# Column-tiled products, paired stores and earlier x in a batched matrix product on one core

## The chip, the cores and the metric

The kernel runs on one NeuronCore of a Trainium2 chip. The metric is device time in microseconds (us) of that core for one execution, as the median of several runs. Lower is better. Instruction times are given in nanoseconds (ns) where they are short.

## The reference

```python
batch, dim_i, dim_j, dim_k = 32, 256, 512, 384
out = np.einsum('bij,bjk->bik', x, y).astype(np.float32)   # x: 32x256x512, y: 32x512x384, float32
```

For each of 32 batches a 256x512 matrix is multiplied by a 512x384 matrix. x is 16.8 MB, y 25.2 MB and the output 12.6 MB, 54.5 MB in all.

## The kernel before, in words

**Operands.** TensorE contracts over the partitions, so j has to lie in the partitions for both operands. y comes that way from memory. x comes with i in the partitions and is transposed on TensorE, four batches at a time (a group, `Q = 4`), with an identity matrix, into PSUM (`t_ps`). Both operands are rounded to fp16 for the product. The j index is dealt out with a stride: partition q of y holds the four rows 4q to 4q+3 of a batch, so that each partition reads one contiguous run of 6 KB, and the transposes take the matching columns of x (`t::NJ`). For x, the 1024 rows of four batches are dealt out eight per partition, a run of 16 KB in each. For the output, partition m holds rows 2m and 2m+1 of one batch, a run of 3 KB.

**Functions.** `load(b)` (L59) issues the DMA of y for one batch (L69, 768 KB) and, for every fourth batch, first the DMA of x for that batch and the next three (L63, 2 MB). `transpose(q)` (L71) makes 32 transposes of 128x128 (L84) in eight sets of four. Each set fills one bank of `t_ps` and is copied to `xt_sb` as fp16, alternately by VectorE (L92) and by ScalarE (L94). `round_y(b)` (L97) copies y to fp16 in four pieces of 128x384, two on ScalarE (L102) and two on VectorE (L104). `multiply(b)` (L106) makes eight matmuls of 128x128 by 128x384 (L115), four for each of two output tiles `o_ps`. `collect(b)` (L124) copies the two tiles to `o_sb`, one on ScalarE (L128) and one on VectorE (L130). `store(b)` (L133) issues the DMA of one batch of output (L135, 384 KB).

**Order.** One Python loop writes the order of every engine's program by hand, one step for each batch (L141). A step s holds: the load of batch s+6, `collect(s-2)`, `multiply(s-1)`, the transposes of a group if s is a multiple of four, `round_y(s)`, and `store(s-2)`. Each engine runs its own part of this list strictly in that order. All DMAs are issued by SyncE (SP), so a load of a later step stands behind the store of the step before it. The framework gives the DMAs eight completion semaphores in rotation. A DMA is issued only when the DMA eight places before it has landed.

**Buffers.** There are 3 buffers for x, 10 for y, 4 for rounded y, 2 for transposed x, 10 for outputs, and in PSUM 4 banks for transposes and 4 for products.

Of the kernel before, what the change touches and what calls it, by code (L numbers as in the profile page):

```python
# [1 line left out]

# [5 lines left out]


MM_DT = mybir.dt.float16  # L10
F32 = mybir.dt.float32
P = 128


Q = 4

LAG = 8

ON_ACT = ()


@with_exitstack
def kernel(
    ctx: ExitStack,
    tc: tile.TileContext,
    x: bass.AP,
    y: bass.AP,
    out: bass.AP,
):
    nc = tc.nc  # L30

    B, I, J = x.shape
    _, _, K = y.shape

    NI = I // P
    NJ = J // P


    R = Q * NI
    PQ = P // Q  # L40

    const_pool = ctx.enter_context(tc.tile_pool(name="const", bufs=1))
    x_pool = ctx.enter_context(tc.tile_pool(name="x_pool", bufs=3))
    y_pool = ctx.enter_context(tc.tile_pool(name="y_pool", bufs=10))
    yr_pool = ctx.enter_context(tc.tile_pool(name="yr_pool", bufs=4))
    xt_pool = ctx.enter_context(tc.tile_pool(name="xt_pool", bufs=2))
    o_pool = ctx.enter_context(tc.tile_pool(name="o_pool", bufs=10))
    tpsum_pool = ctx.enter_context(tc.tile_pool(name="tpsum", bufs=4, space=bass.MemoryType.PSUM))
    opsum_pool = ctx.enter_context(tc.tile_pool(name="opsum", bufs=4, space=bass.MemoryType.PSUM))


    keep = tc.keep_in_program_order

    identity = const_pool.tile([P, P], F32)
    make_identity(nc, identity)

    x_of, y_of, yr_of, xt_of, ps_of, o_of = {}, {}, {}, {}, {}, {}

    def load(b):  # L59
        if b % Q == 0:  # L60
            x_of[b // Q] = x_pool.tile([P, R, J], F32, name="x_sb")
            keep(
                nc.sync.dma_start(  # L63
                    out=x_of[b // Q],
                    in_=x[b : b + Q].rearrange("g (p r) j -> (g p) r j", r=R),
                )
            )
        y_of[b] = y_pool.tile([P, NJ, K], F32, name="y_sb")
        keep(nc.sync.dma_start(out=y_of[b], in_=y[b].rearrange("(q t) k -> q t k", q=P)))  # L69

    def transpose(q):  # L71

        x_sb = x_of.pop(q)
        xt_of[q] = xt_pool.tile([P, Q, NJ, NI, PQ, Q], MM_DT, name="xt_sb")
        n = 0
        for t in range(NJ):
            for e in range(NI):  # L80
                t_ps = tpsum_pool.tile([P, Q, Q, PQ], F32, name="t_ps")
                for h in range(Q):
                    keep(
                        nc.tensor.transpose(  # L84
                            t_ps[:, h].rearrange("c g p -> c (g p)"),
                            x_sb[:, h * NI + e, t::NJ],
                            identity,
                        )
                    )
                dst = xt_of[q][:, :, t, e].rearrange("c g p h -> c h g p")  # L90
                if n % 2 == 0:
                    keep(nc.vector.tensor_copy(dst, t_ps))  # L92
                else:
                    keep(nc.scalar.copy(dst, t_ps))  # L94
                n += 1

    def round_y(b):  # L97
        y_sb = y_of.pop(b)
        yr_of[b] = yr_pool.tile([P, NJ, K], MM_DT, name="y_r")
        for t in range(NJ):  # L100
            if t % 2 == 0:
                keep(nc.scalar.copy(yr_of[b][:, t], y_sb[:, t]))  # L102
            else:
                keep(nc.vector.tensor_copy(yr_of[b][:, t], y_sb[:, t]))  # L104

    def multiply(b):  # L106
        xt_sb, y_r = xt_of[b // Q][:, b % Q], yr_of.pop(b)
        ps_of[b] = [
            opsum_pool.tile([P, K], F32, name=f"o_ps_{e}", tag="o_ps")
            for e in range(NI)  # L110
        ]
        for t in range(NJ):
            for e in range(NI):
                keep(
                    nc.tensor.matmul(  # L115
                        ps_of[b][e],
                        xt_sb[:, t, e].rearrange("c p h -> c (p h)"),
                        y_r[:, t],
                        start=(t == 0),
                        stop=(t == NJ - 1),  # L120
                    )
                )

    def collect(b):  # L124
        o_of[b] = o_pool.tile([P, NI, K], F32, name="o_sb")
        for e in range(NI):
            if e % 2 == 0:
                keep(nc.scalar.copy(o_of[b][:, e], ps_of[b][e]))  # L128
            else:
                keep(nc.vector.tensor_copy(o_of[b][:, e], ps_of[b][e]))  # L130
        del ps_of[b]

    def store(b):  # L133
        eng = nc.scalar if b in ON_ACT else nc.sync
        keep(eng.dma_start(out=out[b].rearrange("(m e) k -> m e k", m=P), in_=o_of.pop(b)))  # L135


    ahead = LAG - 2
    for b in range(ahead):
        load(b)  # L140
    for s in range(B + 2):  # L141
        if s + ahead < B:
            load(s + ahead)
        if s >= 2:
            collect(s - 2)
        if 1 <= s <= B:
            multiply(s - 1)
        if s < B and s % Q == 0:
            transpose(s // Q)
        if s < B:  # L150
            round_y(s)
        if s >= 2:
            store(s - 2)


# [1 line left out]
_INS = ['x', 'y']  # L157
_OUTS = [((32, 256, 384), 'float32')]


# [23 lines left out]
```

## Time and profile before

| what | value |
|---|---|
| median of 8 runs | 136.34 us (136.09 to 136.47) |
| the profiled execution: its own time | 136.15 us |
| the profiled execution: span from first to last instruction | 134.4 us |
| data moved | 54.53 MB in 72 DMAs, 406 GB/s over the span |
| packets of the data queue | 10368, their time is 98.1% of 16 DMA engines' span |
| busy: TensorE matmul, ScalarE, VectorE | 64%, 59%, 54% |

The span is 1.75 us shorter than the profiled execution's own time, which also holds what lies before the first and after the last recorded instruction. A busy share is an average over the whole span. The line of DMA digits gives the share of the 16 DMA engines that was at work in each fortieth of the span. In the list of queues, a packet is one contiguous run moved by one of the 16 DMA engines; runs of 4 bytes are the engines' completion marks, 16 for each DMA.

### The profile page before, as it was taken

How to read it: one execution, taken by the hardware profiler on the slowest of the kernel's cores; microseconds unless marked ns; L12 is line 12 of the kernel's file. 1: busy time of each engine (PE TensorE's matmuls, PEld its weight loads, DVE VectorE, ACT ScalarE, POOL GpSimd, SP SyncE). 2: the span in 40 equal slices, each digit the busy share in tenths (PEclk: the TensorE clock that was granted, in tenths of full speed). 3: DMA queues.
4: the chain of work that ended last, by engine and by line, in shares of the span. 5: the costliest groups of instructions: out<-in, count | busy, mean ns of one | idle time of the engine just before them, and what ended most of it. 6: DMA issues, size and time to landing. Idle time of an engine off the chain costs nothing.

```text
span 134.4 us, 1539 instructions
## 1 busy us (share of the span) xinstructions
PE 86.5 (64%) x512; PEld 64.3 (48%) x512; DVE 73.2 (54%) x128; ACT 79.6 (59%) x129; POOL 0.7 (1%) x6
## 2 busy tenths in 40 slices
PE   0049499869667809769195895949259492785900
PEld 0049358635654409644195454825159250883500
DVE  0007955976497404966078371977028870497610
ACT  3006994996399503996059770998009990289710
POOL 2000000000000000000000000000000000000000
PEclk9999999999999995999959599999968999689997
DMA  4999999999999999999999999999999999999993
GB/s 107 424 402 419 448 411 419 423 440 407 412 417 449 432 396 419 423 437 422 408 422 428 448 424 406 420 416 448 416 409 419 423 462 399 415 424 412 414 414 125
DMA packets 10375, 54.62 MB, mean 406 GB/s; under 512 B 1152, under 2 KB 1152, under 8 KB 9344
## 3 DMA queue, kind: packets, MB, share of 16 engines
q1 hardware_dynamic: 10368, 54.53, 98.1%
q8 instruction: 4, 0.07, 0.2%
q14 instruction: 3, 0.02, 0.0%
HBM read 41.94 MB, written 12.58 MB: 406 GB/s over the span
## 4 chain that ended last, share of the span: by engine, by line
DMA 86%; PE 5%; issue 1%; SPq 1%; DVE 1%; ACT 0%; DVEq 0%
DMA y_sb<-in_y_dram 47%; DMA x_sb<-in_x_dram 21%; DMA out_dram<-o_sb 19%; PE o_ps L115 4%; PE t_ps L84 1%; SPq L69 1%; ACT y_r L102 0%; DVE o_sb L130 0%; SPq L63 0%; DVE y_r L104 0%; SPq L135 0%; DVEq L130 0%
## 5 line engine op out<-in xcount | busy, mean ns | idle before, releaser
L94 ACT CAST xt_sb<-t_ps 128x512 f16<-128x512 f32 x32 | 39.4, 1370 | 44.1 <-PE t_ps L84 43.9
L92 DVE CAST xt_sb<-t_ps 128x512 f16<-128x512 f32 x32 | 39.6, 1331 | 41.0 <-PE t_ps L84 41.0
L84 PE MATMUL t_ps<-identity,x_sb 128*128 128x128 f32 x256 | 41.8, 330 | 25.7 <-DMA x_sb<-in_x_dram 25.7
L115 PE MATMUL o_ps<-y_r,xt_sb 128*128 128x384 f16 x256 | 44.9, 334 | 15.5 <-ACT y_r L102 15.5
L84 PEld LDWEIGHTS t_ps<-identity,x_sb 128*128 128x128 f32 x256 | 39.3, 215 | 29.2 <-issue 27.9
L115 PEld LDWEIGHTS <-xt_sb 128*128 128x128 f16 x256 | 25.7, 100 | 33.8 <-issue 19.0
L102 ACT CAST y_r<-y_sb 128x384 f16<-128x384 f32 x64 | 30.2, 528 | 1.3 <-DMA y_sb<-in_y_dram 1.3
L130 DVE COPY o_sb<-o_ps 128x384 f32<-128x384 f32 x32 | 17.8, 556 | 13.2 <-PE o_ps L115 13.2
L104 DVE CAST y_r<-y_sb 128x384 f16<-128x384 f32 x64 | 19.9, 354 | 0.9 <-DMA y_sb<-in_y_dram 0.9
L128 ACT COPY o_sb<-o_ps 128x384 f32<-128x384 f32 x32 | 15.5, 484 | 2.4 <-PE o_ps L115 2.4
L94 ACT ACT_TABLE_LOAD x1 | 1.3, 1283 | 0.7 <-PEq L168 0.7
masks.py:199 POOL TENSOR_SCALAR_AFFINE_SELECT identity<-identity 128x128 f32<-128x128 f32 x1 | 0.3, 294 | 0.1
masks.py:197 POOL MEMSET identity<- 128x128 f32 x1 | 0.2, 205 | 0.3 <-POOLq L168 0.3
L168 POOL MEMSET const-bfloat16-1.0<- 128x1 bf16 x1 | 0.1, 102 | 0.0
L168 POOL MEMSET const-uint8-127<- 128x1 uint8 x1 | 0.1, 102 | 0.0
L168 POOL MEMSET const-float32-0.0<- 128x1 f32 x1 | 0.1, 99 | 0.2 <-issue 0.2
L168 POOL MEMSET const-float32-1.0<- 128x1 f32 x1 | 0.1, 99 | 0.0
## 6 DMA issues: line engine op xcount, KB each, us to landing
y_sb<-in_y_dram SPq DMA_DIRECT2D x32, 768.0 KB, 15.0
x_sb<-in_x_dram SPq DMA_DIRECT2D x8, 2048.0 KB, 14.2
out_dram<-o_sb SPq DMA_DIRECT2D x32, 384.0 KB, 14.1
```

The costliest lines, as they stand in the source:

```text
L69: keep(nc.sync.dma_start(out=y_of[b], in_=y[b].rearrange("(q t) k -> q t k", q=P)))
L84: nc.tensor.transpose(t_ps[:, h].rearrange("c g p -> c (g p)"), x_sb[:, h * NI + e, t::NJ], identity,)
L92: keep(nc.vector.tensor_copy(dst, t_ps))
L94: keep(nc.scalar.copy(dst, t_ps))
L102: keep(nc.scalar.copy(yr_of[b][:, t], y_sb[:, t]))
L104: keep(nc.vector.tensor_copy(yr_of[b][:, t], y_sb[:, t]))
L115: nc.tensor.matmul(ps_of[b][e], xt_sb[:, t, e].rearrange("c p h -> c (p h)"), y_r[:, t], start=(t == 0), stop=(t == NJ - 1),)
L128: keep(nc.scalar.copy(o_of[b][:, e], ps_of[b][e]))
L130: keep(nc.vector.tensor_copy(o_of[b][:, e], ps_of[b][e]))
L168: nc = _bacc.Bacc("TRN2", target_bir_lowering=False, num_devices=1)
```

## The change

The kernel now works in units of two batches (`G = 2`), so that the loop has 16 steps instead of 32, with `LAG = 4` units.

- **Products** are made for two batches side by side. An output tile of 128 partitions holds 64 partitions of one batch above 64 of the other. Each matmul has 64 columns of weights and writes 64 partitions; two matmuls in a row go to the two halves of the same PSUM bank. There are 512 matmuls of 64 columns instead of 256 of 128, and four tiles for each unit.
- **Stores** take two batches in one DMA of 768 KB, with a run of 6 KB in each partition instead of two stores with runs of 3 KB.
- **Loads** of y take two batches in one DMA of 1.5 MB, except in the first and the last unit, which keep two single loads. x of a group is loaded with the last unit of the group before, ahead of its y, which is two batches sooner in the queue than before. x of the first group is loaded after the y of batch 0.
- **Transposes** of a group are made at the end of the step before the group's first unit, after that step's `round_y`. Those of the first group are made in step 0. Their layout differs: a set holds two output tiles with two row sets each, and the copy to `xt_sb` writes with a step of 2 elements over 128 positions instead of a step of 4 over runs of 32.
- **Buffers** hold two batches each, and their number is halved: 5 for y, 2 for rounded y, 5 for outputs.

```diff
-LAG = 8
+G = 2
+LAG = 4
...
+    def load(u):
+        if (u + 1) * G % Q == 0 and u + 1 < U:
+            load_x((u + 1) * G // Q)
+        y_of[u] = y_pool.tile([P, G, NJ, K], F32, name="y_sb")
+        n = 1 if u in (0, U - 1) else G
+        for g in range(0, G, n):
+            b = u * G + g
...
+                    out=y_of[u][:, g : g + n],
+                    in_=y[b : b + n].rearrange("g (q t) k -> q g t k", q=P),
...
+            if b == 0:
+                load_x(0)
...
-        xt_of[q] = xt_pool.tile([P, Q, NJ, NI, PQ, Q], MM_DT, name="xt_sb")
+        xt_of[q] = xt_pool.tile([P, NJ, NE, Q * PQ, H], MM_DT, name="xt_sb")
...
-                dst = xt_of[q][:, :, t, e].rearrange("c g p h -> c h g p")
+                dst = xt_of[q][:, t, e : e + 2].rearrange("c f p h -> c f h p")
...
+        for e in range(NE):
+            o_ps = opsum_pool.tile([P, K], F32, name="o_ps")
+            ps_of[u].append(o_ps)
+            for t in range(NJ):
+                for g in range(G):
+                    a = (u * G + g) % Q
...
+                            o_ps[g * M : (g + 1) * M],
+                            xt_sb[:, t, e, a * PQ : (a + 1) * PQ].rearrange("c p h -> c (p h)"),
+                            y_r[:, g, t],
...
+                out=out[u * G : (u + 1) * G].rearrange("g (m e) k -> (g m) e k", e=NE),
...
+    for s in range(U + 2):
+        if s + ahead < U:
+            load(s + ahead)
+        if s == 0:
+            transpose(0)
         if s >= 2:
             collect(s - 2)
-        if 1 <= s <= B:
+        if 1 <= s <= U:
             multiply(s - 1)
-        if s < B and s % Q == 0:
-            transpose(s // Q)
-        if s < B:
+        if s < U:
             round_y(s)
+        if (s + 1) * G % Q == 0 and s + 1 < U:
+            transpose((s + 1) * G // Q)
         if s >= 2:
             store(s - 2)
```

## The prediction

> **What bounds the kernel now.** I read the slices of the page first, then its queues and its chain.
>
> ```profile
> DMA  4999999999999999999999999999999999999993
> GB/s 107 424 402 419 448 411 419 423 440 407 412 417 449 432 396 419 423 437 422 408 422 428 448 424 406 420 416 448 416 409 419 423 462 399 415 424 412 414 414 125
> DMA packets 10375, 54.62 MB, mean 406 GB/s; under 512 B 1152, under 2 KB 1152, under 8 KB 9344
> q1 hardware_dynamic: 10368, 54.53, 98.1%
> q8 instruction: 4, 0.07, 0.2%
> DMA 86%; PE 5%; issue 1%; SPq 1%; DVE 1%; ACT 0%; DVEq 0%
> ```
>
> The DMA engines are full in all but the first and last slice. The chain is 86% DMA. So the waits of TensorE for x, 25.7 us in the list of waits, cost nothing: what they delay isn't what the queue lacks. The end is a sum of packet times, plus a head before the queue runs and a tail after it empties. The windows view (columns: stretch, length, busy time and count of PE, PEld, DVE, ACT, POOL, then clock, DMA share, GB/s) gives the rate by kind of traffic.
>
> ```profile
> 4.00:19.00 15.00, 8.38 (x48) 7.15 (x49) 7.02 (x11) 7.75 (x11) 0.00 (x0) 1.00 1.01 427
> 69.00:85.00 16.00, 12.58 (x69) 8.86 (x67) 9.36 (x17) 10.35 (x17) 0.00 (x0) 0.83 1.02 424
> 129.00:130.00 1.00, 0.00 (x0) 0.00 (x0) 0.00 (x0) 0.00 (x0) 0.00 (x0) 1.00 1.03 415
> 131.00:132.00 1.00, 0.00 (x0) 0.00 (x0) 0.00 (x0) 0.00 (x0) 0.00 (x0) 1.00 0.70 283
> ```
>
> Almost only loads: 427. Loads and stores in turn: 424. Stores alone, with their 3 KB runs: 415. Nothing here runs far from the rest. SP's timeline shows the period of a group of four batches by its x issues.
>
> ```profile
> 36.45 0.33 SPq L63 DMA_DIRECT2D x_sb<-in_x_dram  x1
> ...
> 52.47 0.33 SPq L63 DMA_DIRECT2D x_sb<-in_x_dram  x1
> ...
> 84.64 0.33 SPq L63 DMA_DIRECT2D x_sb<-in_x_dram  x1
> ...
> 100.66 0.33 SPq L63 DMA_DIRECT2D x_sb<-in_x_dram  x1
> ```
>
> That is 16.05 us a group (64.21 over four), for 6.82 MB, hence 425 GB/s. By the end of the chain, the products of the last four batches run in one piece and the last copy ends at 128.3, while the queue is full to 131:
>
> ```profile
> 122.36 5.37 PE o_ps L115 x32
> 127.73 0.02 issue
> 127.76 0.56 DVE o_sb L130
> ```
>
> [...] the packet records have medians of 611, 234, 121 and 9 ns for 16 KB, 6 KB, 3 KB and a completion mark. From 3 KB to 6 KB it is 113 ns, so 8 ns of each data packet are fixed. [...] The trace of before has no tiled product. [...] The copies of L92 and L94 write 2 bytes in steps of 8[...] and still take 1331 and 1370 ns against 556 and 484 ns for 384 elements of L130 and L128; the trace shows the step to be dear. [...] four fetches of 16 KB on q8 for 1024 TensorE instructions.
>
> **The change part by part.**
>
> *Stores in runs of 6 KB, fewer DMAs.* 4096 packets of 3 KB become 2048 of 6 KB: 4096 x 121 - 2048 x 234 = 16.4 us of engine time, over 16 engines 1.02 us. DMAs go from 72 to 42, which takes away 480 marks of 9 ns, 0.27 us. The face value is -1.3 us. But packets overlap: stores alone fill 103%. By the landings in the trace a 3 KB store takes 0.945 us, two of them 1.89, and a y load with 6 KB runs 1.885. If a 6 KB store costs what a y load costs, the gain is 16 x 0.005 = 0.1 us. If it keeps the overlap of about 4 ns a packet, it is 8 x 230 + 9 = 1.85 us, and the gain 0.6 us. Against this: x 4.90 us, four y of 1.885 and four stores of 0.945 make 16.22, and the group takes 16.05. The turns from store to load win 0.17 us, four in a group, and the change leaves two: up to 8 x 0.085 = 0.7 us given back. Merged y loads save 14 of the marks, 0.13 us, already in the 0.27. Together -1.3 to +0.6; I take -0.25 us, since 0.6 + 0.27 - 0.7 is about -0.2 and the face value pulls down.
>
> *Products.* A full product is issued every 167 ns in a run (5.37 us for 32). A unit of two batches needs 16 now, 2.7 us, and 32 narrow ones later. If two run at once, 2.7 us again; if not, 5.4 us. Weight loads, 100 ns for 128 columns, become two narrower ones per pair, between 2 x 50 and 2 x 100 ns. I take 170 ns a pair, bounds 167 and 334. In mid-run a unit has 8.0 us of DMA time and TensorE also has 2.7 us of transposes for it (half of 5.4), so even 5.4 fits, barely; the queue covers it. At the end it does not (below).
>
> *Copies out of PSUM.* Counts of y copies and output copies are the same. The transposed copies write in steps of 4 bytes: between the 1331 ns of now and 741 ns (556 x 512/384). I take 1331; nothing depends on it in mid-run, as ScalarE's 5.8 us per unit lie under 8.0 us of DMA.
>
> *x two batches sooner, transposes a step sooner.* Per group one x DMA moves past two y in SP's queue; bytes and number stay. What stood behind x waits 4.9 us longer, and that is y that ScalarE and VectorE round in the step before the transposes. The TensorE waits for x go; next late is the same full queue, so this is worth 0. At the start y of batch 0 comes ahead of x and the first transposes shift from 8.7 to about 10.5 us; the first stores have ten batches of load ahead of them in the queue, over 30 us, so it costs 0 (bounds -0.3 and +0.3, for the order of the first packets).
>
> *Added waits.* Four output banks hold one unit only, so a product waits for the copy of the unit before, and behind it stand TensorE's next transposes. SP's loads still stand behind stores. At such a point three later loads are queued, over 5 us of work after the longest series of copies, and eight larger DMAs may be outstanding: 0.
>
> *Instructions.* TensorE goes from 1024 to 1536 instructions, hence about six fetches instead of four. Each took about 1.0 us on one DMA engine and made that engine about 1.1 us later than the rest in the landings. So far each hit another engine; then two more cost 0. If two meet on one engine: +1.1.
>
> *The end.* Call T the landing of the last y. Behind it are five stores of 1.89 us: the queue ends at T+9.4. On the other side: y of the last unit is rounded by T+1.35 (four casts of about 0.5 on ScalarE, two of them earlier), the copy that frees its first bank ends at T+1.85, products 2.7, last copy 0.6: the store is issued at T+5.2. An issue takes 1.0 us to its first packet (0.74 to 1.73 at the start), 1.9 to move and 0.3 to land: T+8.4. That hides by 1.0 us. A second chain: copies of the last transposes end at about T-4.5, and from T-4 three units of products follow: T-4 + 3m + 0.7 + 3.2. It reaches T+9.4 when a unit takes m = 3.2 us, 198 ns a pair.
>
> Sum: 136.15 - 0.25 = 135.9 for the profiled execution; its median stands 0.19 higher: 136.1 us.
>
> **The rivals.**
>
> *Narrow products don't overlap fully* (slower). Price: from 198 ns a pair on, three times the excess. At 250 ns m = 4.0 and the end comes 2.4 us later, 138.5; at 334 ns m = 5.4 and 6.6 us later, 142.7. [...] Against: full products hide loads of 100 ns now, and quicker copies would start the chain 2 us sooner.
>
> *Two instruction fetches on one DMA engine*: 136.1 + 1.1 = 137.2. For it: six fetches instead of four. Against: the four were spread.
>
> *Face value*: all of the packets' fixed time is won, 136.34 - 1.3 = 135.0. Against: 6 KB loads are no faster than 3 KB stores.
>
> *The stores aren't longer*: if a packet were cut at 3 KB, only marks would go, less the lost turns, 136.6. Against: y has 6 KB packets.
>
> **How the numbers follow.** Forecast 0.59 (own range 135.3 to 136.7), narrow products 0.20, fetches 0.10, face value 0.06, uncut gain absent 0.05. A measurement of this kernel can tell about 0.2%, 0.27 us, from no change. The forecast's gain of 0.25 lies at that bound: of its 0.59, faster 0.28, same 0.24, slower 0.07. With the rivals: faster 0.34, same 0.24, slower 0.42. The range 135.2 to 138.6 leaves out some 0.06 below and 0.1 above.
>
> **What would show it.** Right: data packets of 6 KB at about 230 ns, a group period of 15.9 to 16.1 us, DMA digits still 9 to the last two slices, no wait for x on TensorE, a unit's products within 3.2 us. Wrong: DMA digits that fall before the last store, a unit's products of 4 us or more, one DMA engine landing over 2 us after the others, or a period clearly off 16 us.

## The result, and the profile after

| | before | after |
|---|---|---|
| median | 136.28 us (31 runs beside these) | 137.27 us (136.78 to 137.59, 11 runs) |
| ratio to before, 95% interval | | 1.0070 (1.0059 to 1.0081) |
| the profiled execution: its own time, span, difference | 136.15, 134.4, 1.75 us | 136.97, 134.9, 2.07 us |

The changed kernel is about 1.0 us slower where 0.25 us faster was forecast. Part of that, 0.3 us, lies outside the span.

From the page of the changed kernel, the lines that answer to those of before:

```profile
DMA  4999999999999999999999999999999999999992
GB/s 153 450 393 462 395 421 434 456 380 415 284 459 405 414 426 425 446 408 414 425 429 463 394 417 426 451 415 405 423 425 443 428 403 425 423 428 417 420 397 109
DMA packets 7848, 54.64 MB, mean 405 GB/s; under 512 B 672, under 2 KB 672, under 8 KB 6816
q1 hardware_dynamic: 7840, 54.53, 97.6%
q8 instruction: 6, 0.10, 0.3%
q14 instruction: 2, 0.02, 0.0%
```

The queue is still full throughout, and the packets are as many as reckoned: 6144 of 6 KB, 1024 of 16 KB, 672 marks. But look at the eleventh value of the second line: 284 GB/s in a slice whose DMA digit is 9. There the engines were at work and moved two thirds of the usual bytes; the 6 KB packets that start between 35.0 and 35.5 us took 541 ns on average, against 234. The windows view shows that place in both kernels, first before, then after (the last two columns are DMA share and GB/s).

```profile
33.00:37.00 4.00, 2.79 (x20) 2.26 (x19) 1.59 (x2) 1.11 (x2) 0.00 (x0) 1.00 1.01 415
```

```profile
33.00:37.00 4.00, 1.18 (x9) 1.11 (x9) 2.76 (x7) 3.00 (x6) 0.00 (x0) 1.00 1.01 303
...
53.00:69.00 16.00, 10.94 (x99) 9.61 (x99) 7.25 (x17) 7.58 (x16) 0.00 (x0) 0.93 1.01 424
69.00:85.00 16.00, 11.13 (x100) 9.46 (x99) 7.11 (x17) 7.61 (x17) 0.00 (x0) 0.92 1.01 426
...
129.00:130.00 1.00, 0.00 (x0) 0.00 (x0) 0.28 (x1) 0.00 (x0) 0.00 (x0) 1.00 0.83 344
130.00:131.00 1.00, 0.00 (x0) 0.00 (x0) 0.00 (x0) 0.00 (x0) 0.00 (x0) 1.00 1.00 418
```

In mid-run the rate is that of before: 424 and 426. The trace also records when each of the 16 DMA engines finished its share of a DMA, without naming the engine; these records are called the landings below, and "first" and "last engine" are the first and the last of the 16. By the first engine, the x loads of the fourth and the eighth group land 64.14 us apart (43.47 and 107.61). Before it is the same 64.14 us (48.68 and 112.82), so 16.03 us a group in both. At 129 us the share dips to 0.83: DMA engines that run ahead have nothing left until the last store arrives (it is issued at 129.34, and the first engine lands the store before it at 129.79). The engine that lands last isn't among them: it lands the last two stores at 132.04 and 133.86, 1.82 us apart, no more than the stores before them.

The parts that the forecast had sized on the compute side, first the groups of before, then those of the changed kernel:

```profile
L115 PE MATMUL o_ps<-y_r,xt_sb 128*128 128x384 f16 x256 | 44.9, 334 | 15.5 <-ACT y_r L102 15.5
L94 ACT CAST xt_sb<-t_ps 128x512 f16<-128x512 f32 x32 | 39.4, 1370 | 44.1 <-PE t_ps L84 43.9
L92 DVE CAST xt_sb<-t_ps 128x512 f16<-128x512 f32 x32 | 39.6, 1331 | 41.0 <-PE t_ps L84 41.0
```

```profile
L132 PE MATMUL o_ps<-y_r,xt_sb 128*64 128x384 f16 x512 | 46.5, 339 | 6.0 <-DVE o_sb L147 4.3
L132 PEld LDWEIGHTS <-xt_sb 128*64 128x64 f16 x512 | 36.3, 114 | 15.8 <-issue 7.1
L109 ACT CAST xt_sb<-t_ps 128x512 f16<-128x512 f32 x32 | 22.6, 737 | 20.6 <-PE t_ps L101 20.6
L107 DVE CAST xt_sb<-t_ps 128x512 f16<-128x512 f32 x32 | 22.7, 733 | 20.7 <-PE t_ps L101 20.7
```

and from its chain, the last unit:

```profile
124.74 0.04 DVE y_r L120
...
125.89 2.81 PE o_ps L132 x32
128.69 0.02 issue
128.72 0.56 DVE o_sb L147
```

512 products of 64 columns are busy for 46.5 us where 256 of 128 columns took 44.9, and a unit's 32 run in 2.81 us, 176 ns a pair, against 167 ns for one full product before. So two of them do run at once: in the trace of the last unit the two of a pair start 3 to 4 ns apart, and the pairs, after the first, 162 to 163 ns apart, as single full products did before (median 162 ns). The copies to `xt_sb` fell from 1331 and 1370 to 733 and 737 ns.

### The profile page after: what moved, and what is told of

It reads as the page before. It is cut to its first block, busy times and chain, and to the rows that moved or that the text cites. A ratio compares the mean times of both kernels' runs of the same rounds, so it can differ in the third digit from the quotient of the medians.

```text
span 134.9 us, 1958 instructions
## 1 busy us (share of the span) xinstructions
PE 88.9 (66%) x768; PEld 75.1 (56%) x768; DVE 56.2 (42%) x128; ACT 62.5 (46%) x129; POOL 0.7 (1%) x6
## 4 chain that ended last, share of the span: by engine, by line
DMA 72%; PE 10%; DVE 6%; SPq 4%; ACT 2%; issue 2%; DVEq 0%; ACTq 0%
DMA y_sb<-in_y_dram 72%; PE t_ps L101 7%; PE o_ps L132 3%; DVE y_r L120 3%; DVE xt_sb L107 2%; SPq L66 2%; SPq L82 2%; ACT o_sb L145 1%; DVE o_sb L147 1%; SPq L152 1%; ACT xt_sb L109 0%; DVEq L120 0%; ACTq L145 0%
## 5 line engine op out<-in xcount | busy, mean ns | idle before, releaser
L101 PE MATMUL t_ps<-identity,x_sb 128*128 128x128 f32 x256 | 42.6, 333 | 33.7 <-DVE xt_sb L107 20.0
L101 PEld LDWEIGHTS t_ps<-identity,x_sb 128*128 128x128 f32 x256 | 38.8, 214 | 37.4 <-DVE xt_sb L107 21.1
L132 PE MATMUL o_ps<-y_r,xt_sb 128*64 128x384 f16 x512 | 46.5, 339 | 6.0 <-DVE o_sb L147 4.3
L118 ACT CAST y_r<-y_sb 128x384 f16<-128x384 f32 x64 | 28.3, 520 | 43.5 <-DMA y_sb<-in_y_dram 43.5
L132 PEld LDWEIGHTS <-xt_sb 128*64 128x64 f16 x512 | 36.3, 114 | 15.8 <-issue 7.1
L120 DVE CAST y_r<-y_sb 128x384 f16<-128x384 f32 x64 | 18.6, 353 | 42.4 <-DMA y_sb<-in_y_dram 42.2
L109 ACT CAST xt_sb<-t_ps 128x512 f16<-128x512 f32 x32 | 22.6, 737 | 20.6 <-PE t_ps L101 20.6
L107 DVE CAST xt_sb<-t_ps 128x512 f16<-128x512 f32 x32 | 22.7, 733 | 20.7 <-PE t_ps L101 20.7
L147 DVE COPY o_sb<-o_ps 128x384 f32<-128x384 f32 x32 | 16.9, 550 | 10.0 <-PE o_ps L132 9.9
L145 ACT COPY o_sb<-o_ps 128x384 f32<-128x384 f32 x32 | 14.1, 493 | 1.2 <-PE o_ps L132 1.2
```

Of the source, the lines that this page charges most:

```text
L101: nc.tensor.transpose(t_ps[:, f, h], x_sb[:, h * NE + e + f, t::NJ], identity)
L118: keep(nc.scalar.copy(yr_of[u][:, g, t], y_sb[:, g, t]))
L120: keep(nc.vector.tensor_copy(yr_of[u][:, g, t], y_sb[:, g, t]))
L132: nc.tensor.matmul(o_ps[g * M : (g + 1) * M], xt_sb[:, t, e, a * PQ : (a + 1) * PQ].rearrange("c p h -> c (p h)"), y_r[:, g, t], start=(t ...
L145: keep(nc.scalar.copy(o_of[u][:, e], ps_of[u][e]))
L147: keep(nc.vector.tensor_copy(o_of[u][:, e], ps_of[u][e]))
```

## The experiments

Three theories were set against each other. The **fetch theory**: two more TensorE instruction fetches make one DMA engine late. The **stall theory**: the slow packets at 33 to 37 us are the loss. The **end theory**: the last store comes too late. Each kernel was compared with the kernel before on the same chip; medians of that were 136.28 to 136.30.

**again.** The changed kernel, unchanged.

> The changed kernel unchanged, to see which parts of its profile repeat. Stall theory: the slow packets at 33 to 37 us (about 1.1 us of extra packet time on every DMA engine) belong to the kernel and are there again, at the same place. Chance: they are gone, and the time then falls to 136.3 or less. Fetch theory: six instruction fetches again, and the slowest DMA engine lands over 2 us after the fastest, with or without the slow packets. Time 137.0 to 137.5.

Measured: 137.23 (ratio 1.0079, 1.0060 to 1.0099). Slow packets at the same place, six fetches, the last landing 2.4 us after the first for the second last store. The slow packets belong to the kernel.

**b_yfirst.** The kernel before with y of batch 0 ahead of x.

```diff
     def load(b):
+        if b == 0:
+            y_of[b] = y_pool.tile([P, NJ, K], F32, name="y_sb")
+            keep(nc.sync.dma_start(out=y_of[b], in_=y[b].rearrange("(q t) k -> q t k", q=P)))
         if b % Q == 0:
...
-        y_of[b] = y_pool.tile([P, NJ, K], F32, name="y_sb")
-        keep(nc.sync.dma_start(out=y_of[b], in_=y[b].rearrange("(q t) k -> q t k", q=P)))
+        if b > 0:
+            y_of[b] = y_pool.tile([P, NJ, K], F32, name="y_sb")
+            keep(nc.sync.dma_start(out=y_of[b], in_=y[b].rearrange("(q t) k -> q t k", q=P)))
```

> The kernel before with one thing changed: y of batch 0 is loaded ahead of the first x. In the landings the fastest DMA engine of the changed kernel had lost 2.4 us to the head instead of 2.9. If the order of the first two loads does that, this kernel is 0.4 to 0.6 us faster than before; if it is chance or due to something else, no difference.

Measured: 136.56 (1.0016, 1.0003 to 1.0029), with a wide spread, from 135.84 to 137.07. The expectation failed, and showed why: the tenth DMA lands 0.52 us sooner on the first engine (27.29 against 27.81), and by the nineteenth that is gone (43.76 against 43.81). Between them, y packets between 32 and 36 us average 271 ns against 237 in the kernel before. So the order of two DMAs brings slow packets into a kernel that had none. The windows view of this kernel, where the kernel before has 415 GB/s:

```profile
33.00:37.00 4.00, 4.00 (x29) 3.19 (x28) 2.58 (x5) 2.06 (x5) 0.00 (x0) 1.00 0.99 376
```

**b_extra_pe.** The kernel before with 512 more TensorE instructions: 256 small products, each with its weight load.

```diff
+        for t in range(NJ):
+            for e in range(NI):
+                keep(
+                    nc.tensor.matmul(
+                        ps_of[b][e][:, :32],
+                        xt_sb[:, t, e].rearrange("c p h -> c (p h)"),
+                        y_r[:, t, :32],
+                        start=True,
+                        stop=True,
+                    )
+                )
```

> The kernel before with 256 extra small products (32 columns) into banks that the real products then overwrite: 1536 TensorE instructions and so six instruction fetches instead of four, as in the changed kernel, with loads, stores and order untouched. TensorE has over a third of its time free. Fetch theory: 0.5 to 1.2 us slower than before, and the slowest DMA engine lands more than 2 us after the fastest. Stall theory and end theory: no difference.

Measured: 136.52 (1.0015, 1.0007 to 1.0024), six fetches, no slow packets. Slower by 0.24 us, below the expected band. The two more fetches (or the other effects of those products, which this run doesn't separate) cost this much here, a quarter of what the changed kernel lost.

**a_fullwidth.** The changed kernel with full-width products; the transposed layout and the products of before, the rest as changed.

```diff
+        for g in range(G):
+            a = (u * G + g) % Q
+            for e in range(2):
+                o_ps = opsum_pool.tile([P, K], F32, name="o_ps")
+                ps_of[u].append(o_ps)
+                for t in range(NJ):
+                    keep(
+                        nc.tensor.matmul(
+                            o_ps,
+                            xt_sb[:, a, t, e].rearrange("c p h -> c (p h)"),
+                            y_r[:, g, t],
...
-                out=out[u * G : (u + 1) * G].rearrange("g (m e) k -> (g m) e k", e=NE),
-                in_=o_of.pop(u),
+                out=out[u * G : (u + 1) * G].rearrange("g (m e) k -> m g e k", e=2),
+                in_=o_of.pop(u).rearrange("m (g e) k -> m g e k", e=2),
```

> The changed kernel with the products made at full width again (256 of 128 columns, the transposed layout of before), units of two batches, loads, order and buffers as changed. A store is still one DMA of two batches, with two runs of 3 KB in each partition. 1024 TensorE instructions, four fetches. Fetch theory: 0.5 to 1 us faster than the changed kernel, near 136.3. Stall theory (the start with 12 MB of loads before any store): stays near 137.2, with slow packets at 33 to 37 us. End theory (last store issued late): stays near 137.2, with the DMA digits falling before the last store.

Measured: 137.53 (1.0085, 1.0067 to 1.0103), four fetches, slow packets as before. So neither two more fetches nor narrow products are the main loss: without both the kernel is no faster. The run doesn't price them by themselves, since its stores are back at runs of 3 KB.

**a_xfirst.** The changed kernel with x ahead of y of batch 0.

```diff
+        if u == 0:
+            load_x(0)
         y_of[u] = y_pool.tile([P, G, NJ, K], F32, name="y_sb")
...
-            if b == 0:
-                load_x(0)
```

> The changed kernel with x of the first group loaded ahead of y of batch 0 again, and nothing else. Order theory (y first is what makes the DMA engines meet slow packets when y of batches 8 and 9 is loaded): no slow packets at 33 to 37 us, the head 0.5 us later, and 0.2 to 0.5 us faster than the changed kernel, 136.7 to 137.0. Unit theory (they come from the 12 MB of loads in a row): slow packets stay and the time rises to 137.5 or more.

Measured: 136.40 (1.0007, 0.9996 to 1.0017), 0.85 us faster than the changed kernel, more than expected. No slow packets at 33 to 37 us, by the windows view of this kernel:

```profile
33.00:37.00 4.00, 1.22 (x8) 1.02 (x7) 2.43 (x6) 2.84 (x6) 0.00 (x0) 0.80 1.01 416
```

By this one edit, the order of the first two loads is most of the loss.

**a_y1.** The changed kernel (y first) with y loads of one batch.

```diff
-        n = 1 if u in (0, U - 1) else G
+        n = 1
```

> The changed kernel with every y load for one batch again: 56 DMAs, seven for each semaphore, instead of 42. Epilogue theory: the 56th DMA is on the last semaphore, so SP's final waits end with the last landing (0.05 us from landing to the end waits instead of 0.25), and SP's longer program meets its instruction fetch during the run and not after the end (time outside the span 1.75 instead of 2.05): about 0.5 us faster, 136.7 to 136.8. If the time outside the span has nothing to do with SP's program: it stays at 2.05, and the gain is 0.2 at most. Slow packets stay.

Measured: 136.99 (1.0055, 1.0039 to 1.0070). The time outside the span went from 2.07 to 1.76 us in the median of the runs, as the epilogue theory had it, and from the last landing to the end of the span from 1.00 to 0.83 us. The gain in the median is 0.26 us, half of what was expected: in this profile the last engine is 3.0 us behind the first from 36 us on, against 2.3 to 2.5 in the changed kernel, which may have taken the rest back.

**a_y1_xfirst.** Both of the above.

> Both of the above: x first, and y loads for one batch. If the two theories hold and add up, 136.2 to 136.6, within 0.3 us of the kernel before; what is left is the two more TensorE instruction fetches (0.24 us in the run with extra products). If it stays above 136.9, another cause is missing.

Measured: **136.03** (0.9986, 0.9975 to 0.9997), below the expected band and faster than the kernel before. It is the fastest of all kernels tried.

**b_74.** The kernel before with two y loads cut in two.

```diff
+        src = y[b].rearrange("(q t) k -> q t k", q=P)
+        if b in (20, 21):
+            keep(nc.sync.dma_start(out=y_of[b][:, : NJ // 2], in_=src[:, : NJ // 2]))
+            keep(nc.sync.dma_start(out=y_of[b][:, NJ // 2 :], in_=src[:, NJ // 2 :]))
+        else:
+            keep(nc.sync.dma_start(out=y_of[b], in_=src))
```

> The kernel before with the y loads of batches 20 and 21 cut in two DMAs each: 74 DMAs instead of 72, the same bytes, so that the last DMA falls on the second of the eight completion semaphores. Epilogue theory: SP waits for it first and then goes through the others, 0.2 us slower (136.45 to 136.5), with more waits between the last landing and the end of the span (1.04 us instead of 0.83). Otherwise: no difference.

Measured: 136.55 (1.0018, 1.0004 to 1.0031), 0.25 us slower. From the last landing to the end of the span it is 1.00 us (134.03 to 135.03) against 0.83. The sign is as expected; 0.17 us of it is in the final waits, and the rest could be the two more DMAs with shorter runs. SP's list of waits shows the two endings, first of the kernel before, then of b_74:

```profile
SPq L179 <- DMA out_dram<-o_sb: 4.7, 5, 1.1
```

```profile
SPq L184 <- DMA out_dram<-o_sb: 4.6, 1, 4.6
```

Before, SP waits five times for one store after the other, and the last landing ends it. In b_74 one wait of 4.6 us holds the last landing, and SP goes through three more semaphores after it, about 0.06 us each. The changed kernel does the same, and has the same 1.00 us. (The expectations gave 1.04 us for it, from a rounded span.)

**a_rev.** The changed kernel (y first), groups taken from memory in reverse order; shown for y, x and the output go the same way.

```diff
             b = u * G + g
+            c = (B // Q - 1 - b // Q) * Q + b % Q
...
-                    in_=y[b : b + n].rearrange("g (q t) k -> q g t k", q=P),
+                    in_=y[c : c + n].rearrange("g (q t) k -> q g t k", q=P),
```

> The changed kernel, y first, with the groups of four batches taken in reverse order from memory: the fifth y load then reads batches 20 and 21, not 8 and 9, and all else is as it was. Address theory (those rows of y are slow to read in that state): the slow packets of 33 to 37 us go or move. Place theory (it is this point of the stream, whatever is read): y packets still take about 290 to 310 ns on average between 32 and 36 us, against 234 later. Time about 137.2 in the second case, 136.4 to 136.7 in the first.

Measured: 136.95 (1.0057, 1.0037 to 1.0077). Slow packets at 34 to 36 us, up to 561 ns on average in half a microsecond. Which rows are read is not the cause.

**a_pad.** The changed kernel with one useless load of 768 KB near the start.

```diff
+            if b == 1:
+                pad = pad_pool.tile([P, NJ, K], F32, name="pad")
+                keep(nc.sync.dma_start(out=pad, in_=y[0].rearrange("(q t) k -> q t k", q=P)))
```

> The changed kernel, y first, with one more load of 768 KB that nothing uses, after y of batch 1: everything behind it comes 1.9 us later in the stream. Stream theory: the slow packets come with the load of batches 8 and 9, now at 35.5 to 39 us. Clock theory (something at a fixed time after the start): they stay at 33 to 37 us, on other loads. Time about 139.1 in both.

Measured: 139.21 (1.0213, 1.0197 to 1.0229). The slow packets came at 35.5 to 37.5 us, 1.9 us later, again in the load of batches 8 and 9. The clock theory falls.

**a_late_store.** The changed kernel with the first store behind one more unit of loads.

```diff
-        if s >= 2:
+        if s == 3:
+            store(0)
+        if s >= 3:
             store(s - 2)
```

> The changed kernel, y first, with the first store issued one unit later, behind the loads of x of the fourth group and of y of batches 10 and 11. First-store theory (the slow packets hit the load that stands right before the first store): y of batches 8 and 9 is read at 234 to 240 ns a packet, and the slow packets come some 8.7 us later, with batches 10 and 11, at 42 to 46 us. Place theory (it is the end of the first run of loads, whatever follows): they stay at 33 to 37 us. Time 137.0 to 137.5 in both.

Measured: 136.93 (1.0061, 1.0039 to 1.0083). The slow packets moved with the store, by the windows view of this kernel:

```profile
33.00:37.00 4.00, 3.47 (x28) 3.11 (x25) 2.75 (x7) 3.00 (x6) 0.00 (x0) 1.00 1.07 445
...
42.00:45.00 3.00, 3.00 (x36) 2.44 (x31) 0.31 (x1) 0.04 (x1) 0.00 (x0) 1.00 1.02 347
```

445 GB/s where the changed kernel had 303, and 347 at 42 to 45 us, where batches 10 and 11 are loaded. So the slow packets are again in the load right before the first store. The store itself was issued only 2.3 us later than in the changed kernel (28.59 against 26.30 us); what moved by one unit is its place in the queue, and the slow packets went with the place.

**a_full_y1_x.** The kernel a_y1_xfirst with the full-width products and 3 KB runs of a_fullwidth (the same edits, not repeated).

> The kernel with x first and single y loads, but with full-width products and runs of 3 KB in the stores: 1024 TensorE instructions and four fetches. It holds against that one what the column tiling is worth by itself. If 6 KB runs are worth their face value, it is 1.0 us slower, 137.0. If they are worth about 0.3 us and the two more fetches cost 0.25, no difference: 135.9 to 136.2.

Measured: 136.43 (1.0016, 1.0007 to 1.0025), 0.40 us slower than a_y1_xfirst, between the two expectations. So narrow products with 6 KB runs gain 0.40 us net, together with their two more fetches.

**a_x2.** a_y1_xfirst with the first x in two DMAs of 8 KB runs.

```diff
-        keep(
-            nc.sync.dma_start(
-                out=x_of[q],
-                in_=x[q * Q : (q + 1) * Q].rearrange("g (p r) j -> (g p) r j", r=R),
-            )
-        )
+        src = x[q * Q : (q + 1) * Q].rearrange("g (p r) j -> (g p) r j", r=R)
+        n = R // 2 if q == 0 else R
+        for r in range(0, R, n):
+            keep(nc.sync.dma_start(out=x_of[q][:, r : r + n], in_=src[:, r : r + n]))
```

> The kernel with x first and single y loads, with x of the first group loaded by two DMAs of 8 KB runs (and y of batches 14 and 15 by one, to keep 56 DMAs). If the 0.5 us that y first saved at the head come from shorter first packets, about half of it is won without the slow packets: 135.7 to 135.9. If shorter first packets are themselves what brings the slow packets, 136.3 to 137.

Measured: 136.36 (1.0006, 0.9993 to 1.0020), 0.33 us slower than a_y1_xfirst, with slow packets at 34 to 36 us of about half the size. So y as such isn't needed: a first DMA of x with shorter runs brings slow packets too, fewer of them. (Two y loads of batches 14 and 15 are merged in this run, to keep 56 DMAs.)

## Why the prediction was wrong

**The step that failed** is the one on the start: "the first stores have ten batches of load ahead of them in the queue, over 30 us, so it costs 0 (bounds -0.3 and +0.3, for the order of the first packets)". The reasoning looked at who waits, and nobody does. The runs showed 0.85 us: 137.25 with y first (between 137.27 and 137.23, the two medians of the changed kernel), 136.40 with x first. Among the kernels with single y loads the same order costs 0.96 us (136.99 and 136.03), and in the kernel before only 0.28 (b_yfirst), so its price depends on the kernel.

The order saves less than it loses. In the landings of the changed kernel the first engine is 0.56 us ahead after the head (32.17 for the eighth DMA, 32.73 in a_xfirst), the last engine only 0.16 us. The next DMA, the load of two batches ahead of the first store, takes 4.51 us on the first engine and 5.30 us on the last, against 3.76 and 3.72 in a_xfirst. So the first engine loses 0.75 us and the last 1.58 us, and the last engine ends the program. Counted above 234 ns each, the 6 KB packets that start between 20 and 50 us cost every engine 1.29 us on average in the changed kernel, 1.00 in its second run and 0.28 in a_xfirst, a difference of the size of the loss. That the slow packets go with the load before the first store, and not with time or the rows, is shown by a_pad, a_rev and a_late_store.

That they account for all of the 0.85 us isn't shown: it is a difference of medians, and the last landings of the two profiled executions are only 0.13 us apart. The profiled execution of a_xfirst took 136.85 us, 0.45 above its median, and in it the last engine loses another 0.5 us near the end, on one store (2.31 us where the others take 1.82 to 1.88), with an instruction fetch at 126.4 us just before.

**What stays open** is why a first DMA with shorter runs does this. In the y-first profiles the last two engines land the first DMA 0.83 to 1.2 us after the first engine, in a_x2 0.87 and 1.11, in the other x-first ones 0.5 to 0.8. So the slow packets go with engines that fall apart at the start; whether the one causes the other is not shown. One could guess that engines which already store disturb those that still load. The record speaks against it. Where stores have packets of 3 KB, they can be told from loads: in a_fullwidth 35 of the 36 packets over 350 ns between 28 and 38 us start before the first store packet (36.18 us), in b_yfirst 18 of 25 (33.91 us).

**A second term was missing**: what the number of DMAs does to the end of the program. With y loads of one batch, a_xfirst became a_y1_xfirst and won 0.37 us, where the forecast had 0.13 us in favour of merging. With y first it was 0.26. Two causes can be seen. The 72 DMAs of before, and 56, end on the last of eight semaphores and 42 don't, so SP goes through other waits after the last landing: from landing to the end of the span 1.00 us against 0.83. And the time outside the span is 1.92 to 2.12 us in the seven profiles whose page shows two fetches on q14, and 1.77 to 1.86 us in the eight that show three or four; the medians are about 2.0 and 1.8. The page of a_y1_xfirst:

```profile
q8 instruction: 6, 0.10, 0.3%
q14 instruction: 3, 0.02, 0.0%
```

With 42 DMAs SP has 75 recorded instructions, with 56 it has 89, with 72 it has 121. In the trace the third fetch comes at 97.8 us before, at 132.3 us in a_y1_xfirst, and at 136.7 us, behind the end of the span, in the changed kernel. That this fetch is SP's, and that it makes the 0.2 to 0.3 us, fits all fifteen profiles, but was not tried by itself.

**The steps that held.** *The packets*: -0.25 us was forecast for the body of the change. With the two losses undone, a_y1_xfirst stands at -0.27 us by the medians (ratio 0.9986, so -0.19 us); narrow products with longer runs gain 0.40 us net, with the fetches and the quicker transposed copies in it. The face value of 1.3 us was rightly cut down. In mid-run the landings show none of the gain (64.14 us for four groups in both kernels); that the lost turns took it back there, as the forecast had it, fits this but was not tried by itself. At the end, where only stores are left, a 6 KB store takes the last engine 1.83 us (1.85 was reckoned with the overlap kept) and two 3 KB stores took 1.89; over five stores that is 0.3 us. *Products*: 170 ns a pair forecast, 176 measured; the rival of products that don't overlap is out. That two would run at once was the author's estimate: the trace of before, without a tiled product, shows neither this nor the contrary. *The last unit*: from T, 124.71, the last store was forecast at T+5.2 and issued at T+4.6. It hides on the engine that ends, but not on the first ones, which stood still; the forecast had taken the engines as one. *Transposed copies*: 733 ns, just under the lower bound of 741, worth nothing as said. *Waits for x* went but for a rest: five waits of 13.8 us are left in all, 10.2 of them before the first transpose. *Group period*: 16.03 us, within the 15.9 to 16.1 named.

Of the signs of being wrong that were named, one came: the last engine lands 2.3 to 2.5 us after the first, where 2 us was the limit; the kernel before was already at 2.0. It had been meant for two fetches on one engine. In the changed kernel the lag grows from 0.85 to 1.7 us at the first fetch, as it did before (0.7 to 1.8), and to 2.5 us in the load with the slow packets.

**The rival of the fetches** forecast 137.2, the time that was measured, but for the wrong reason: the two more fetches are worth 0.24 us in b_extra_pe, and with four fetches a_fullwidth is no faster. That its figure was hit is luck.

**The sum**, in medians: +0.85 for the order of the first loads, +0.37 for merged loads with what they do to the end, -0.27 for all else, in all +0.95, against 0.95 to 0.99 measured. This is a way of dividing the difference and no independent proof: the last term is what was left over, and undone in the other order the first two are 0.26 for merging and 0.96 for the order.

## What to carry to other kernels

In this kernel, whose DMA queue is always full, the last of the DMA engines set the end (its last landing is at 133.86 us of a span of 134.9). In one like it, look at slow stretches in the rate where the DMA digits are still 9, and not only at waits. The order of the first two loads was worth 0.3 to 1 us here though nothing waits for them: try it alone before it is mixed with other changes. And when the number of DMAs changes, look at the end: which wait of SP holds the last landing, and whether an instruction fetch has moved behind the span.

## What was not expected of the hardware

- Packets of 6 KB took up to 580 ns on average over half a microsecond (a_pad), against 234, in the load ahead of the first store, if the program's first DMA had runs of 6 KB. Over the 4 us from 32 to 36 they averaged 271 ns in b_yfirst and 315 in the changed kernel; with a first DMA of 16 KB runs it was 237 to 244 ns.
- The fetches of 16 KB on q8, four for 1024 TensorE instructions and six for 1536, took 0.95 to 1.06 us each on a DMA engine before and 0.90 to 1.08 us after. 512 more instructions, two more fetches, made a kernel with free TensorE time 0.24 us slower (b_extra_pe).
- Writing 2-byte elements in steps of 4 bytes over 128 positions, instead of 8 bytes over runs of 32, took a copy of 128x512 from PSUM from 1331 to 733 ns on VectorE and from 1370 to 737 ns on ScalarE.
- A weight load of 64 columns took 114 ns on average in the changed kernel, one of 128 columns 100 ns before.
